# Prompt attention of a hybrid decoder step: mask products in the rounded type, and value products two score blocks behind

## The chip, the cores and the metric

The kernel runs on one core of a Trainium2 chip. The metric is the device time of one execution in microseconds. The kernel before took 2216.69 us (median of three runs, 2213.21 to 2216.88).

## The reference

One decoder layer is computed for a prompt of 1024 tokens and for 8 sequences of 8 new tokens that attend to 8192 cached ones each. The part that the change touches is the causal attention of the prompt, 8 heads with query and key width 96 (64 + 32 rotary) and value width 64, in float32:

```python
s = jnp.einsum('bqhd,bkhd->bhqk', qi, k, preferred_element_type=jnp.float32) * MLA_SCALE
qpos = start + jnp.arange(Q_BLOCK)
s = jnp.where(kpos[None, :] <= qpos[:, None], s, NEG)
pr = jax.nn.softmax(s, axis=-1)
return jnp.einsum('bhqk,bkhd->bqhd', pr.astype(v.dtype), v)
```

Beside it the step has a gated linear attention, a latent attention of the 64 new tokens over the paged cache, an output projection, a gated MLP with a short convolution and a last gated projection.

## The kernel before, in words

**Precision.** A float32 factor is kept as two halves of a rounded 32-bit type that TensorE multiplies in one pass: `split` (L114 to L117) rounds on ScalarE (L115) and subtracts on VectorE or GpSimd (L116). A product is the sum of three (`mm3`, L138 to L141): high by high, low by high, high by low.

**Stages.** Up to about 640 us the prompt's projections and its gated linear attention run; from there to about 1053 us the prompt attention; then the output projection, the MLP and the last projection. Beside all of the first two runs the *cache stream* (`cache_stream`): 64 blocks of 1024 cached tokens, in each of which TensorE transposes the latents (L522, tile `ctp`), multiplies them into keys for 8 heads and the absorbed queries (L139 to L141, tile `ks`: two groups of three products for 128 tokens), ScalarE squares the keys (L560, `csq`) and copies scores (L562, `sn`), VectorE sums (L565), GpSimd scales, and TensorE sums the values (L646, `cpv`).

**What sets the order.** The cache stream and the dense work are Python generators. The dense one yields costs, the main loop draws a cache step each time that its due time is reached (`PACE`), and 95 cache steps are drawn before the dense work ends, in the kernel before and in the changed one. The remaining cache steps are drawn together with the output projection. What is recorded in this way is then ordered on each engine by a scheduler when the program is built; an engine then works through its queue in that order, and the first instruction that waits holds all behind it.

**Prompt attention.** It has 16 units: a head `h` and a half `g` of 512 queries. `prepare` makes a unit's operands: `operands` turns q and k (L1263) for a new head, `shifts` multiplies scores once in the high halves (L1279), adds the mask of the diagonal block as a product of an identity with a mask matrix (L1281) and takes the row maximum on VectorE (L1282), `rows` turns the maxima into an extra row of q (L1292). `values` then goes over blocks `j` of 128 keys, 4 of them for g = 0 and 8 for g = 1: three score products (L1308, L1309, L1312) into the tile `S`, with the mask product (L1311) in the four diagonal blocks, the exponential on ScalarE (L1316, `p`), the rounded half `ph` on VectorE or ScalarE in turn (L1317), the rest `pl` on GpSimd (L1318), and one block later the products with the values into `o`: L1323, L1324 (from `ph`) and L1326 (from `pl`); the first block's `pl` comes last, in L1330. `both` draws the values of one unit and the preparation of the next in turn. The tiles `t`, `S` and `o` of the attention share three PSUM banks (`psD`) with the other dense work.

The mask products go over 16 units x 4 diagonal blocks, twice: 64 in L1281 and 64 in L1311, 128 in all. Their factors are in bfloat16, those of all the products around them are of the rounded type.

Of the kernel before, what the change touches and what calls it, by code (L numbers as in the profile page):

```python
# [8 lines left out]
F32 = mybir.dt.float32  # L9
F32R = mybir.dt.float32r  # L10
BF16 = mybir.dt.bfloat16
I32 = mybir.dt.int32
AF = mybir.ActivationFunctionType
ALU = mybir.AluOpType
# [4 lines left out]
P = 128  # L19
# [16 lines left out]
NEG = -1e30  # L36
# [8 lines left out]
def step_kernel(ctx: ExitStack, tc: tile.TileContext, A):  # L45
    nc = tc.nc
    pe, act, dve, pool, sp = nc.tensor, nc.scalar, nc.vector, nc.gpsimd, nc.sync
# [9 lines left out]
    ident = ctile([P, P], F32, "ident")  # L57
# [131 lines left out]
    def pat(kind):  # L189
        return psD.tile([P, 512], F32, tag="d", name=kind)  # L190
# [1035 lines left out]
    def prompt_attention(ap):  # L1226
# [9 lines left out]
            return ld  # L1236

        ld = {0: load(0)}
        identb = ap.tile([P, P], BF16, name="identb", tag="identb", bufs=1)
        pool.tensor_copy(identb, ident)  # L1240
        masks = []
        for nm, sg in (("maskq", 1), ("maskk", -1)):
            m = ap.tile([P, P], BF16, name=nm, tag=nm, bufs=1)
            pool.memset(m, 0.0)
            pool.affine_select(m, m, pattern=[[-sg, P]], compare_op=ALU.is_ge, fill=NEG, base=0, channel_multiplier=sg)
            masks.append(m)
        maskq, maskk = masks
        qk, vo = [], []
# [20 lines left out]
        def shifts(h, g):  # L1269
            tr = qk[h % 2]  # L1270
            mx = ap.tile([P, 4, 2], F32, tag="amx", name="amx")
            for ii in range(4):
                i = 4 * g + ii
                qs = slice(i * P, (i + 1) * P)
                for j in range(g + 1):
                    kw = (ii + 1) * P if j == g else 512
                    S = pat("t")
                    k0 = j * 512
                    pe.matmul(S[:, 0:kw], tr["qh"][0:96, qs], tr["kh"][0:96, k0:k0 + kw], start=True, stop=j < g)  # L1279
                    if j == g:  # L1280
                        pe.matmul(S[:, kw - P:kw], identb, maskq, start=False, stop=True)  # L1281
                    dve.tensor_reduce(mx[:, ii, j:j + 1], S[:, 0:kw], AX.X, ALU.max, negate=True)  # L1282
                yield 0.06 * (i + 1)
            if g == 1:
                dve.tensor_tensor(mx[:, :, 0], mx[:, :, 0], mx[:, :, 1], ALU.min)
            return mx
# [9 lines left out]
        def values(h, g):  # L1296
            tr = qk[h % 2]
            v = vo[h % 2]
            o = pat("o")
            nj = 4 * g + 4  # L1300
            pls, q = {}, []
            for j in range(nj + 1):
                if j < nj:
                    c0 = max(0, j - 4 * g) * P
                    ks = slice(j * P, (j + 1) * P)
                    qs = slice(g * 512 + c0, g * 512 + 512)
                    S = pat("S")
                    pe.matmul(S[:, c0:], tr["kh"][:, ks], tr["qh"][:, qs], start=True, stop=False)  # L1308
                    pe.matmul(S[:, c0:], tr["kh"][:, ks], tr["ql"][:, qs], start=False, stop=False)  # L1309
                    if j >= 4 * g:  # L1310
                        pe.matmul(S[:, c0:c0 + P], identb, maskk, start=False, stop=False)  # L1311
                    pe.matmul(S[:, c0:], tr["kl"][:, ks], tr["qh"][:, qs], start=False, stop=True)  # L1312
                    p = ap.tile([P, 512], F32, tag="p", name="p", bufs=3)
                    ph = ap.tile([P, 512], F32R, tag="ph", name="ph", bufs=3)
                    pl = ap.tile([P, 512], F32R, tag="pl" if j else "pl0", name="pl", bufs=3 if j else 2)
                    act.activation(p[:, c0:], S[:, c0:], AF.Exp)  # L1316
                    (dve.tensor_copy if j % 2 else act.copy)(ph[:, c0:], p[:, c0:])  # L1317
                    pool.tensor_tensor(pl[:, c0:], p[:, c0:], ph[:, c0:].bitcast(F32), ALU.subtract)  # L1318
                    q.append((j, c0, ph, pl))
                    yield 0.65  # L1320
                if j > 0:
                    jj, c0, ph, pl = q.pop(0)
                    pe.matmul(o[:, c0:], v[:, jj, 0:128], ph[:, c0:], start=jj == 0, stop=False)  # L1323
                    pe.matmul(o[0:64, c0:], v[:, jj, 128:192], ph[:, c0:], start=False, stop=False)  # L1324
                    if jj > 0:
                        pe.matmul(o[:, c0:], v[:, jj, 0:128], pl[:, c0:], start=False, stop=False)  # L1326
                    else:
                        pl0 = pl
                    yield 0.6
            pe.matmul(o, v[:, 0, 0:128], pl0, start=False, stop=True)  # L1330
            r = ap.tile([64, 512], F32, tag="ar", name="ar")
            act.activation(r, o[64:128, :], AF.Ln)
            act.activation(r, r, AF.Exp, scale=-1.0)
            dve.tensor_tensor(r, o[0:64, :], r, ALU.mult)
            sp.dma_start(doT[512 + h * 64:512 + (h + 1) * 64, g * 512:(g + 1) * 512], r)
            yield 0.2
# [926 lines left out]
```

## Time and profile before

| | us |
|---|---|
| runs, median (lowest to highest) | 2216.69 (2213.21 to 2216.88) |
| profiled execution, first to last instruction | 2211.1 |
| TensorE busy in it | 2126.7 (96%) |
| VectorE, ScalarE, GpSimd busy | 1668.4, 1366.7, 1233.9 |
| mask products, first to last | 656.8 to 1047.5 |

The page gives for the profiled execution only its span; the runs' times include what lies before the first and behind the last instruction, so their median lies 5.6 us above the span. A matmul's row in the profile is longer than its share of the engine, since matmuls overlap: what one costs is read from the distance of the starts.

### The profile page before, as it was taken

Reading aid. Unit: us, or ns where it says so; the run is one execution under the profiler, and the core shown is the slowest. Engines: PE = TensorE matmul, PEld = TensorE weight load, DVE = VectorE, ACT = ScalarE, POOL = GpSimd, SP = SyncE. Lnnn points to the kernel's source line nnn. Section 1 sums busy time; section 2 is a strip of 40 time slices with the busy share of each in tenths; the row PEclk is TensorE's granted clock in tenths of the full one; section 3 lists DMA queues with packets and bytes.
Section 4 is the critical chain, followed back from the end, with each engine's and each line's share of the span. In section 5 each row is a group of like instructions: output and inputs, shape, how many; then the busy total and the mean of one; then the engine's idle time right before and its main releaser. Section 6 shows DMA issues by size and latency. Waiting matters only on the chain.

```text
span 2211.1 us, 38379 instructions
## 1 busy us (share of the span) xinstructions
PE 2126.7 (96%) x13460; PEld 1927.2 (87%) x13460; DVE 1668.4 (75%) x2551; ACT 1366.7 (62%) x3724; POOL 1233.9 (56%) x1330
## 2 busy tenths in 40 slices
PE   7999989999999999999999997999999999999999
PEld 6889978878888888887898875999999999888899
DVE  4775667467788888887888788888888886887642
ACT  5676766777778888887777766333333333534631
POOL 5675668576777777778455557756566562011100
PEclk9999999999999999999999998999999999999999
DMA  5343235412342222221522222332232325777321
GB/s 185 106 144 108 78 119 156 141 54 69 105 120 61 63 74 61 61 56 46 171 77 69 74 77 82 101 102 90 92 95 91 101 91 191 240 218 237 101 71 39
DMA packets 204418, 233.07 MB, mean 105 GB/s; under 512 B 42422, under 2 KB 146339, under 8 KB 204227
## 3 DMA queue, kind: packets, MB, share of 16 engines
q1 hardware_dynamic: 188259, 179.49, 26.0%
q0 software_dynamic: 14736, 46.67, 7.4%
q10 hardware_dynamic: 1232, 4.46, 0.5%
q8 instruction: 108, 1.77, 0.3%
q14 instruction: 83, 0.68, 0.1%
HBM read 188.00 MB, written 42.52 MB: 104 GB/s over the span
## 4 chain that ended last, share of the span: by engine, by line
PE 79%; DVE 7%; ACT 5%; DMA 3%; POOL 3%; issue 2%; SPq 0%; DVEq 0%; POOLq 0%; ACTq 0%
PE ps_gu L140 7%; PE ps_gu L141 7%; PE ps_gu L139 7%; PE ks L139 5%; PE ks L141 4%; PE ks L140 4%; PE ps_dn L140 3%; PE ps_dn L141 3%; PE ps_dn L139 3%; PE cpv L646 2%; PE ctp L522 2%; PE ps_lt L278 2%; PE ps_pj L139 2%; DVE css L565 1%; PE ps_pj L140 1%
## 5 line engine op out<-in xcount | busy, mean ns | idle before, releaser
L560 ACT ACTIVATE csq<-ks 128x256 f32<-128x256 f32 x1040 | 392.7, 400 | 91.1 <-PE ks L141 80.2
L565 DVE TENSOR_REDUCE css<-csq 128x16 f32<-128x1024 f32 (+1 forms) x264 | 315.7, 1196 | 61.2 <-ACT csq L560 58.2
L115 ACT CAST wh<-st 128x512 fp32r<-128x512 f32 x176 | 108.4, 619 | 189.0 <-PE ps_gu L140 168.7
L139 PE MATMUL ks<-mv0h,cTh 128*128 128x320 f32 (+1 forms) x520 | 171.0, 331 | 8.8 <-ACT sn L562 4.6
L139 PE MATMUL ks<-mv1h,cTh 128*128 128x320 f32 (+1 forms) x520 | 169.6, 328 | 7.8 <-ACT sn L562 3.5
L605 POOL TENSOR_TENSOR chl<-craw,chl 128x1024 fp32r<-128x1024 f32 x64 | 141.6, 2213 | 55.2 <-ACT chl L603 53.0
L140 PE MATMUL ks<-mv1l,cTh 128*128 128x320 f32 (+1 forms) x520 | 153.1, 296 | 0.0
L140 PE MATMUL ks<-mv0l,cTh 128*128 128x320 f32 (+1 forms) x520 | 152.0, 294 | 0.0
L141 PE MATMUL ks<-mv0h,cTl 128*128 128x320 f32 (+1 forms) x520 | 147.6, 297 | 0.9 <-DVE cTl L116 0.8
L141 PE MATMUL ks<-mv1h,cTl 128*128 128x320 f32 (+1 forms) x520 | 148.0, 298 | 0.1
L116 DVE TENSOR_TENSOR wl<-st,wh 128x512 fp32r<-128x512 f32 x132 | 119.0, 903 | 26.3 <-ACT wh L115 26.3
L631 POOL TENSOR_TENSOR phl<-sn,phl 128x512 fp32r<-128x512 f32 (+1 forms) x64 | 85.5, 1335 | 84.8 <-ACT phl L630 84.3
L116 POOL TENSOR_TENSOR wl<-st,wh 128x512 fp32r<-128x512 f32 x44 | 69.4, 1578 | 102.9 <-ACT wh L115 102.9
L140 PE MATMUL ps_dn<-o 128*128 128x512 f32 x308 | 120.1, 390 | 0.4 <-DVE o L116 0.4
L141 PE MATMUL ps_dn<-o 128*128 128x512 f32 x308 | 120.2, 390 | 0.0
L116 DVE TENSOR_TENSOR cTl<-ctp,cTh 128x512 fp32r<-128x512 f32 (+1 forms) x136 | 90.0, 662 | 37.8 <-ACT cTh L115 36.8
L139 PEld LDWEIGHTS ks<-mv0h,cTh 128*128 128x128 f32 x520 | 97.9, 188 | 23.2 <-ACT sn L562 9.4
L562 ACT COPY sn<-ks 128x64 f32<-128x64 f32 x520 | 116.7, 224 | 0.0
L139 PEld LDWEIGHTS ks<-mv1h,cTh 128*128 128x128 f32 x520 | 99.0, 190 | 20.1 <-ACT sn L562 7.9
L1318 POOL TENSOR_TENSOR pl<-p,ph 128x512 fp32r<-128x512 f32 (+1 forms) x96 | 97.5, 1020 | 30.3 <-DVE ph L1317 21.2
L139 PE MATMUL ps_dn<-o 128*128 128x512 f32 x308 | 112.1, 390 | 0.0
L141 PE MATMUL ps_gu<-xrh,wl 128*128 128x320 f32 x352 | 108.7, 309 | 0.0
(670 smaller groups left out, 7871.4 us busy)
## 6 DMA issues: line engine op xcount, KB each, us to landing
raw<-ds SPq DMA_DIRECT2D x77, 256.0 KB
raw<-ffn_w_down SPq DMA_DIRECT2D x66, 256.0 KB
stage<-w_in SPq DMA_DIRECT2D x48, 256.0 KB
st<-ffn_w_gate SPq DMA_DIRECT2D x44, 256.0 KB
st<-ffn_w_up SPq DMA_DIRECT2D x44, 256.0 KB
wr<-ffn_w_down SPq DMA_DIRECT2D x44, 256.0 KB
ds<-cv SPq DMA_DIRECT2D x21, 512.0 KB
oraw<-doT SPq DMA_DIRECT2D x16, 256.0 KB
```

The costliest lines, as they stand in the source:

```text
L115: cast = act.copy(hi, src)
L116: res = (lo_eng or dve).tensor_tensor(lo, src, hi.bitcast(F32), ALU.subtract)
L139: pe.matmul(ps, ah, bh, start=first, stop=False)
L140: pe.matmul(ps, ah, bl, start=False, stop=False)
L141: return pe.matmul(ps, al, bh, start=False, stop=last)
L278: pe.matmul(ps, x, w, start=first, stop=last)
L560: act.activation(sq[:, f * 256:f * 256 + 256], ks[:, 0:256], AF.Square)
L562: act.copy(o.sn[:, g0 + i, :], ks[:, 256:320])
L565: dve.tensor_reduce(o.ss[:, g0 + i + 1 - n:g0 + i + 1, :].rearrange("p i h -> p (i h)"), sq2[:, :n].rearrange("p i (h n) -> p (i h) n", n= ...
L605: pool.tensor_tensor(ch[:, c0:c1, 128:256], src, ch[:, c0:c1, 0:128].bitcast(F32), ALU.subtract)
L631: pool.tensor_tensor(phl[:, :nt, 64:128], sb, phl[:, :nt, 0:64].bitcast(F32), ALU.subtract)
L1318: pool.tensor_tensor(pl[:, c0:], p[:, c0:], ph[:, c0:].bitcast(F32), ALU.subtract)
```

## The change

The identity and the two mask matrices become tiles of the rounded type (`identr`, `maskq`, `maskk`). Each mask is first made on GpSimd in a float32 tile `mraw`, of which there is one buffer, and then copied. The mask products themselves stay where they stand in the program. In `values` the loop runs one step further, and a block's value products follow two blocks behind its scores; `ph` and `pl` get four buffers instead of three (`p` keeps three).

```diff
-        identb = ap.tile([P, P], BF16, name="identb", tag="identb", bufs=1)
-        pool.tensor_copy(identb, ident)
+        identr = ap.tile([P, P], F32R, name="identr", tag="identr", bufs=1)
+        pool.tensor_copy(identr, ident)
         for nm, sg in (("maskq", 1), ("maskk", -1)):
-            m = ap.tile([P, P], BF16, name=nm, tag=nm, bufs=1)
-            pool.memset(m, 0.0)
-            pool.affine_select(m, m, pattern=[[-sg, P]], compare_op=ALU.is_ge, fill=NEG, base=0, channel_multiplier=sg)
+            raw = ap.tile([P, P], F32, name="mraw", tag="mraw", bufs=1)
+            m = ap.tile([P, P], F32R, name=nm, tag=nm, bufs=1)
+            pool.memset(raw, 0.0)
+            pool.affine_select(raw, raw, pattern=[[-sg, P]], compare_op=ALU.is_ge, fill=NEG, base=0, channel_multiplier=sg)
+            pool.tensor_copy(m, raw)
...
-                        pe.matmul(S[:, kw - P:kw], identb, maskq, start=False, stop=True)
+                        pe.matmul(S[:, kw - P:kw], identr, maskq, start=False, stop=True)
...
-            for j in range(nj + 1):
+            for j in range(nj + 2):
...
-                        pe.matmul(S[:, c0:c0 + P], identb, maskk, start=False, stop=False)
+                        pe.matmul(S[:, c0:c0 + P], identr, maskk, start=False, stop=False)
...
-                    ph = ap.tile([P, 512], F32R, tag="ph", name="ph", bufs=3)
-                    pl = ap.tile([P, 512], F32R, tag="pl" if j else "pl0", name="pl", bufs=3 if j else 2)
+                    ph = ap.tile([P, 512], F32R, tag="ph", name="ph", bufs=4)
+                    pl = ap.tile([P, 512], F32R, tag="pl" if j else "pl0", name="pl", bufs=4 if j else 2)
...
-                if j > 0:
+                if j > 1:
                     jj, c0, ph, pl = q.pop(0)
```

Lines behind L1247 stand two further down in the changed kernel (L1281 becomes L1283).

The scheduler orders the whole stretch from the first mask product to some way into the output projection anew. Three places on TensorE follow; `ks`, `ctp`, `csr`, `cpv`, `mt` and `crp` are tiles of the cache stream, `ps_dn` of the output projection.

The preparation of the last unit, before: its maxima's score products, while the last unit but one multiplies its values.

```order
L1279 MATMUL t<-kh_9446,qh_9444 128x512
L1279 MATMUL t<-kh_9446,qh_9444 128x256
L1281 LDWEIGHTS identb
L1281 MATMUL t<-maskq,identb 128x128
L1323 MATMUL o<-ph,vo_9448 128x512
L1324 MATMUL o<-ph,vo_9448 64x512
L1279 MATMUL t<-kh_9446,qh_9444 128x512
L1323 MATMUL o<-ph,vo_9448 128x384
L1324 MATMUL o<-ph,vo_9448 64x384
L1279 MATMUL t<-kh_9446,qh_9444 128x384
L1281 LDWEIGHTS identb
L1281 MATMUL t<-maskq,identb 128x128
```

The same place in the changed kernel:

```order
L1281 MATMUL t<-kh_9450,qh_9448 128x512
L139 MATMUL ks<-mv1h,cTh 128x320
L140 MATMUL ks<-mv1l,cTh 128x320
L141 MATMUL ks<-mv1h,cTl 128x320
L139 MATMUL ks<-mv1h,cTh 128x256
L140 MATMUL ks<-mv1l,cTh 128x256
L141 MATMUL ks<-mv1h,cTl 128x256
L1281 MATMUL t<-kh_9450,qh_9448 128x256
L1283 MATMUL t<-maskq,identr 128x128
```

Two groups of cache products now stand between two score products that stood side by side. Over the last three units, counted from one L1330 to the next, the program before has 86, 6 and 9 `ks` products, the changed one 72, 69 and 27. Behind the attention's last product and ahead of the first product of the output projection it had 51 `ks` products and now has 90.

The values of the last unit, before:

```order
L1308 MATMUL S<-qh_9444,kh_9446 128x512
L1309 MATMUL S<-ql_9445,kh_9446 128x512
L1312 MATMUL S<-qh_9444,kl_9447 128x512
L1323 MATMUL o<-ph,vo_9448 128x512
L1324 MATMUL o<-ph,vo_9448 64x512
L1326 MATMUL o<-pl,vo_9448 128x512
```

and in the changed kernel:

```order
L1310 MATMUL S<-qh_9448,kh_9450 128x512
L1311 MATMUL S<-ql_9449,kh_9450 128x512
L1313 MATMUL S<-maskk,identr 128x128
L1314 MATMUL S<-qh_9448,kl_9451 128x512
L1328 MATMUL o<-pl,vo_9452 128x512
L1325 MATMUL o<-ph,vo_9452 128x512
L1326 MATMUL o<-ph,vo_9452 64x512
```

Before, a block's `pl` followed its `ph` in one go, behind the next block's scores; now the `pl` product of one block is followed by the `ph` products of the next, and more score products lie ahead of both.

On GpSimd at the start of the attention, the changed kernel has these rows between the first fills and the cache stream's next large subtraction (L605); before, both masks were filled and cut ahead of L592:

```order
L592 TENSOR_TENSOR sn<-sn,cy 128x512
L116 TENSOR_TENSOR vo_9444<-ldv,vo_9444 128x8x64
L1247 CAST maskq<-mraw 128x128
L631 TENSOR_TENSOR phl<-sn,phl 128x9x64
L594 TENSOR_TENSOR sn<-sn,sr 128x512
L1245 MEMSET mraw 128x128
L1246 AFFINE_SELECT mraw<-mraw 128x128
L1247 CAST maskk<-mraw 128x128
```

Each mask now ends in a copy, and the second is made only when the first has left `mraw`.

## The prediction

> **What bounds the kernel now.** I read the page's busy shares and its chain first, then the stages by windows, then the waits and groups of the stage that the change touches.
>
> ```profile
> PE 2126.7 (96%) x13460; PEld 1927.2 (87%) x13460; DVE 1668.4 (75%) x2551; ACT 1366.7 (62%) x3724; POOL 1233.9 (56%) x1330
> PE 79%; DVE 7%; ACT 5%; DMA 3%; POOL 3%; issue 2%; SPq 0%; DVEq 0%; POOLq 0%; ACTq 0%
> ```
>
> TensorE is busy for 96% of the span, and 79% of the chain that ended last is its own. So a change gains what it takes off TensorE's queue or out of its holes. The share is an average; the attention's own stage is read from windows (columns: length, then busy time of PE, PEld, DVE, ACT, POOL with counts, granted clock, DMA share, GB/s).
>
> ```profile
> 656.00:1018.00 362.00, 355.00 (x2455) 311.24 (x2455) 303.66 (x495) 316.66 (x948) 271.96 (x270) 1.00 0.23 65
> 1000.00:1020.00 20.00, 20.00 (x139) 17.27 (x138) 17.86 (x28) 16.96 (x56) 14.71 (x16) 1.00 0.21 61
> 1020.00:1030.00 10.00, 7.59 (x41) 5.94 (x40) 6.57 (x12) 4.51 (x10) 7.81 (x13) 0.85 0.06 14
> 1030.00:1040.00 10.00, 8.78 (x45) 7.04 (x45) 4.57 (x10) 7.15 (x15) 7.63 (x8) 0.84 0.26 66
> 1040.00:1050.00 10.00, 10.00 (x60) 8.12 (x60) 6.01 (x8) 6.78 (x14) 9.38 (x9) 0.97 0.11 29
> 1052.60:1062.20 9.60, 8.14 (x56) 7.25 (x55) 7.48 (x10) 9.40 (x34) 0.78 (x4) 1.00 0.39 116
> ```
>
> Three things stand here. For 362 us the attention and the cache stream fill TensorE (355.0 of 362.0) at full clock. In the 20 us from 1020 on there is a hole: TensorE is busy for 7.59 + 8.78 of 20 us, and the granted clock is 0.85 and 0.84. That is 3.6 us without work, and 15% or so of 16.4 busy us at a lower clock, some 2.5 us: about 6 us in all. And between the attention's end and the first output product (1052.6 to 1062.2) it is ScalarE that is full, 9.40 of 9.60 us, while TensorE is not.
>
> Who made the hole, from the waits of TensorE in 1018 to 1048 (total, times, longest):
>
> ```profile
> PE t L1279 <- DVE amx L1282: 1.6, 2, 0.8
> PE cpv L646 <- POOL phl L631: 0.8, 1, 0.8
> PE S L1309 <- DVE ql L116: 0.8, 1, 0.8
> PE t L1292 <- DVE amx L1285: 0.4, 1, 0.4
> ```
>
> Score products wait for VectorE's maxima, since their PSUM bank must be read first, and nothing else stands between them: the last three units have 86, 6 and 9 `ks` products beside them. The 95 cache steps drawn by then are used up too early.
>
> **The change part by part.** *The mask products.* What one costs in bfloat16, from the order of time; below it what a product of the rounded type of the same width, 128, costs.
>
> ```profile
> 1043.70 0.39 PE L1309 MATMUL S<-ql,kh 97*128 97x512 f32 x1
> 1043.93 0.23 PE L1311 MATMUL S<-maskk,identb 128*128 128x128 bf16 x1
> 1043.97 0.48 PE L1312 MATMUL S<-qh,kl 97*128 97x512 f32 x1
> 1044.29 0.39 PE L1323 MATMUL o<-ph,vo 128*128 128x512 f32 x1
> 1044.52 0.39 PE L1324 MATMUL o<-ph,vo 128*64 128x512 f32 x1
> 1043.47 0.19 PEld L1309 LDWEIGHTS S<-ql,kh 97*128 97x128 f32 x1
> 1043.93 0.10 PEld L1311 LDWEIGHTS <-identb 128*128 128x128 bf16 x1 [0.27 <-issue]
> 1020.03 0.27 PE L1326 MATMUL o<-pl,vo 128*128 128x128 f32 x1
> 1020.14 0.45 PE L1330 MATMUL o<-pl,vo 128*128 128x512 f32 x1
> ```
>
> A product over 512 columns takes 0.23 us of the engine (1043.70 to 1043.93, 1044.29 to 1044.52). From 1043.93 to 1044.29 there are the mask product and L1312's: 0.36 - 0.23 = 0.13 us for the mask. The reason stands in the weight rows: the load of the bfloat16 identity is not issued ahead (idle 0.27, "issue"), it begins when the product before has streamed. The product of the rounded type over 128 columns takes 0.11 us (1020.03 to 1020.14). So 0.02 x 128 = 2.6 us less. Bounds: if the loads of the new identity stood open too, each would be 0.19 long instead of 0.10, 0.09 x 128 = 11.5 us more; if such a product cost only its stream, a quarter of 0.23, 0.06 us, then 0.07 x 128 = 9 us less. I take -2.6, the nearest row: every load of this type around the place runs under the product ahead of it.
>
> Here a rule speaks against the change. The Trainium skill, TensorE: Matmul & The Clock Gate, section "Weight-path perf modes — Fast Weight Load (FWL) and DoubleRow", says that the fast weight load is on for 128 weights of a type other than FP32, about twice as fast as measured there. The two load rows agree with it, 0.10 against 0.19; what it would make of the time is the second rival.
>
> *The masks' making.* On GpSimd, once:
>
> ```profile
> L1240 POOL CAST identb<-ident 128x128 bf16<-128x128 f32 x1 | 0.5, 498 | 0.0
> L1245 POOL TENSOR_SCALAR_AFFINE_SELECT maskq<-maskq 128x128 bf16<-128x128 bf16 x1 | 0.3, 306 | 0.0
> L594 POOL TENSOR_TENSOR sn<-sn,sr 128x512 f32<-128x512 f32 x1 | 1.3, 1281 | 0.0
> ```
>
> Two copies more, 2 x 0.5 = 1.0 us, beside the same fills and cuts, on an engine with 271.96 of 362 us busy. The first mask is ready later, since L592 and a subtraction of the values (about as long as L594, 1.3 us) now stand ahead of its copy; nine to fifteen cache products, each 0.12 to 0.15 us, have been set ahead of L1283 for it. Between 0 and 1.6 us; I take +0.5. The cover is the cache stream's products; without them TensorE would stand for the whole 1.6 us with three banks held.
>
> *Value products a block later.* What they wait for now, over the attention:
>
> ```profile
> L1323 PEld LDWEIGHTS o<-ph,vo 128*128 128x128 f32 x96 | 18.4, 191 | 3.1 <-DVE ph L1317 1.1 <-DVE ar L1334 0.4 <-ACT p L1316 0.4
> L1326 PEld LDWEIGHTS o<-pl,vo 128*128 128x128 f32 x80 | 15.4, 193 | 1.6 <-POOL pl L1318 0.7
> L1318 POOL TENSOR_TENSOR pl<-p,ph 128x512 fp32r<-128x512 f32 x48 | 62.1, 1297 | 12.5 <-ACT ph L1317 6.6 <-DVE ph L1317 5.5
> L1317 ACT CAST ph<-p 128x512 fp32r<-128x512 f32 x32 | 20.2, 632 | 0.2
> L1317 DVE CAST ph<-p 128x512 fp32r<-128x512 f32 x16 | 12.5, 780 | 4.3 <-ACT p L1316 4.2
> L1316 ACT ACTIVATE p<-S 128x512 f32<-128x512 f32 x48 | 29.0, 604 | 8.5 <-PE S L1312 6.4 <-POOL sn L592 0.9 <-POOL pl L1318 0.2
> ```
>
> Exponential, rounding and subtraction of a wide block take 0.60 + 0.63 to 0.78 + 1.30 = 2.5 to 2.7 us one behind the other. Already the cache products hide nearly all of it: the weight loads of the value products stood idle for 3.1 + 1.6 = 4.7 us in 16 units, and 1.1 + 0.4 + 0.7 = 2.2 us of that is put down to `ph`, `p` and `pl`. All of it gone would be 4.7; a loss is possible, since `o` keeps its bank a block longer and leaves two of three for `t` and `S`: a wait of a unit's length of L1279 <- DVE amx (0.8 us) in a few units, +2. I take -1.5.
>
> *What the new order does to the hole.* The last three units get 72, 69 and 27 `ks` products instead of 86, 6 and 9. 69 products at 0.12 to 0.15 us are some 9 us of cover for the unit in which the hole lies. The last unit stays thinly covered. Of the 6 us I take 5 back; bounds 0 and 7.
>
> *Where the cover comes from.* Behind the attention 90 `ks` products instead of 51 now stand ahead of the output projection's first. There nothing but cache work is in the queue, and ScalarE sets the pace:
>
> ```profile
> L560 ACT ACTIVATE csq<-ks 128x256 f32<-128x256 f32 x16 | 6.0, 398 | 0.0
> L562 ACT COPY sn<-ks 128x64 f32<-128x64 f32 x8 | 1.8, 224 | 0.0
> ```
>
> For six `ks` products ScalarE needs 2 x 0.398 + 0.224 = 1.02 us; TensorE needs 3 x 0.12 + 3 x 0.147 = 0.80 (the cadence of 256 and 320 columns by the 0.23 of 512: 0.115 and 0.144). The 39 products more are 6.5 such sets: 6.5 x 0.22 = 1.4 us by these rows alone. ScalarE also has the transposes' casts and the probabilities there, so it may be double; as the row of 1052.6 to 1062.2 shows, TensorE had 8.14 of 9.60 us, a loss of 15%, and a stretch some 10 us longer would lose 1.5 more. The upper bound is that ScalarE falls behind as well for the output weights' casts: 5. I take +2.5.
>
> Sum: -2.6 + 0.5 - 1.5 - 5 + 2.5 = -6.1 us. Against the profiled execution's span of 2211.1 that makes 2205.0. The median of the runs lies 5.6 us above that span, so 2216.7 - 6.1 = 2210.6 is the time to expect.
>
> **The rivals.** *The cover is only moved.* The hole closes, and the whole 5 us come back in the stretch of pure cache work, where ScalarE is full; the deeper values bring nothing, since scheduled order had given them room already. Left is -2.6 + 0.5 = -2.1: 2214.6. For it: ScalarE's 9.40 of 9.60 us, and 4.5 us of the waits in the attention not being of the values. Against it: in the hole ScalarE had 11.7 of 20 us only, so its work is done earlier there than before.
>
> *The identity's load stands open (slower).* It begins in the attention, at each of the 128 mask products, if the order in which PE's sequencer issues them, and not the type, keeps the load from being issued ahead; then -2.6 becomes +11.5 and the sum is 0.5 - 1.5 - 5 + 2.5 + 11.5 = +8.0: 2224.7. Against it: the loads of L1309 and L1312 directly beside it are under other products. For it only the two lengths.
>
> *A new hole.* The whole stretch is ordered anew; one hole like that of 1020 to 1040 in another place costs 6 us and leaves 2216.6, two leave 2222.6. Against it: no unit ahead of the last has fewer than 45 `ks` products beside it, where the hole had 6 and 9.
>
> *More than I count.* Hole, clock and waits of the values go wholly: -2.6 - 4.7 - 7 + 1.4 = -12.9: 2203.8.
>
> **How the numbers follow.** Forecast 0.52, moved cover 0.22, open loads 0.08, a new hole 0.10, more 0.08. What a measurement of this kernel can tell from no change is about 0.2%, 4.4 us: faster means under 2212.3, slower over 2221.1. The forecast's own range, 2206 to 2214, lies by about nine tenths below 2212.3, 0.47, with the 0.08 of the last and a little of the second rival 0.57. Slower: open loads 0.08 and most of the new hole's, 0.15. The rest, 0.28, is no difference. The range goes from 2202 to 2222: it holds the forecast, the moved cover, one new hole, and nearly all of the greater gain; the open loads lie outside.
>
> **What would show it.** The windows from the attention's last 30 us show TensorE at 9.5 of 10 us or more and a clock of 1.00 if the hole is closed. The starts around L1313 tell the mask's price: 0.11 if I am right, 0.20 or more if the load stands open. The window between the last L1332 and the first L1436 shows the moved cover: ScalarE full and TensorE under 85%. The weight loads' idle time at L1325 and L1328 should fall from 4.7 us to about 3. I am wrong if the hole is closed and the time is within 2 us of before, or if L1281 waits for VectorE in other units for more than the 1.6 us here.

## The result, and the profile after

The changed kernel takes 2220.8 us (median of 20 runs, 2216.3 to 2226.7), the kernel before 2216.2 (20 runs on the same chip, 2212.7 to 2222.5): a ratio of 1.0017, 95% interval 1.0011 to 1.0024. It is slower, by some 4 us, where 6 us less were predicted.

The two profiled executions are not medians: the one of before is 3.0 us below its median, the one of after took 2223.9 us, 3.0 above. So their stages differ by 11 us in sum, not by 4.6, and what a stage shows is confirmed below by timed runs. (The page's span lies some 2 us under the time of its own run; the 5.6 that the prediction, and the section on the time before, took for this was mostly the low run.)

Of the page of after: busy time by engine, and the engines' shares of the chain that ended last.

```profile
PE 2128.3 (96%) x13460; PEld 1940.2 (87%) x13460; DVE 1676.5 (75%) x2551; ACT 1364.7 (61%) x3724; POOL 1233.1 (55%) x1332
PE 78%; DVE 9%; ACT 5%; DMA 3%; POOL 2%; issue 2%; SPq 0%; DVEq 0%; POOLq 0%; ACTq 0%
```

These shares tell nothing: 96% before and after. The windows of after do (length, then busy time of PE, PEld, DVE, ACT, POOL with counts, clock, DMA share, GB/s):

```profile
656.00:1018.00 362.00, 351.55 (x2413) 317.83 (x2413) 302.96 (x489) 306.55 (x911) 264.29 (x265) 1.00 0.22 61
1018.00:1037.30 19.30, 19.23 (x127) 17.00 (x126) 14.47 (x21) 16.60 (x48) 17.29 (x18) 1.00 0.14 42
1037.30:1050.00 12.70, 9.08 (x61) 7.57 (x59) 10.76 (x17) 11.74 (x37) 8.00 (x13) 0.99 0.45 143
1050.00:1060.00 10.00, 3.68 (x17) 3.71 (x18) 1.72 (x3) 1.34 (x5) 2.33 (x2) 0.50 1.01 389
1060.00:1070.70 10.70, 8.75 (x60) 7.66 (x60) 9.42 (x15) 8.50 (x30) 7.14 (x9) 1.00 0.96 290
```

The attention's last 19.3 us are full at full clock: the old hole is closed, as predicted. Its last product now comes at 1037.3 instead of 1052.5. Behind it the stretch up to the first output product lasts 33.4 us instead of 9.8, and in the 10 us from 1050 on TensorE has 3.68 us of work at a clock of 0.50. ScalarE, whose pace the prediction took for the limit there, is busy for 11.74 + 1.34 + 8.50 = 21.6 of the 33.4 us: it is not full. The waits of TensorE from 1037 to 1071 name the cause (total, times, longest):

```profile
PE ctp L522 <- DMA craw<-cache_ckv,idx: 8.6, 2, 8.3
PE ks L139 <- ACT sn L562: 2.4, 3, 1.6
PE ks L139 <- ACT csq L560: 0.8, 1, 0.8
```

Its row in TensorE's timeline (start, length, and in brackets the idle time before it and what ended it):

```profile
1056.32 1.09 PE L522 MATMUL ctp<-ident,craw 128*128 128x128 f32 x4 [8.34 <-DMA craw<-cache_ckv,idx]
```

The gather of the next cache block comes late. GpSimd issues it, and SP's loads for the output projection start at the same time (timelines of GpSimd and of SP's queue, same columns):

```profile
1043.54 1.16 POOL L490 CAST qbd1h<-qr 32x64 fp32r<-32x64 f32 x3 [3.16 <-issue]
1044.78 2.33 POOL L491 TENSOR_TENSOR qbd1l<-qr,qbd1h 32x64 fp32r<-32x64 f32 x4
1047.38 0.97 POOL L473 DMA_INDIRECT craw<-cache_ckv,idx  x1 [0.27 <-POOL qbd1l L491]
1045.87 1.07 SPq L1555 DMA_DIRECT2D h<-x_prompt  x2
1047.94 4.26 SPq L1555 DMA_DIRECT2D h<-x_prompt  x6
```

The view of the tile `craw` from 1000 to 1075 has the time from issue to landing:

```profile
DMA to landing us min/median/max: 4.1/4.9/8.8
```

A gather lands 4.9 us after its issue as a rule, this one after 8.8.

**Where TensorE's time went.** For the experiments one measure is used throughout. A product's own share is worked out from rows like those of the prediction: 0.23 us for 512 columns, so 0.45 ns a column, but not under 0.118 us behind a load of 128 weights (0.136 for a bfloat16 mask). What the distances between successive starts are longer than that, shorter ones set off, is *lost*. A lower granted clock counts as lost too. Summed over five stages of each profiled execution, in us:

| kernel | to 800 | 800 to 1018 | 1018 to attention's end | to the first output product | to the first MLP product | sum |
|---|---|---|---|---|---|---|
| before | 10.9 | 10.8 | 9.0 | 2.5 | 44.6 | 77.8 |
| after | 17.9 | 11.2 | 0.5 | 16.5 | 42.8 | 88.9 |

The hole gave back 8.5. The stretch behind the attention took 14.0, and the attention's first third 7.0, of which nothing stood in the prediction. The products' own shares became some 2 us shorter (cheaper masks).

The measure is rough. Taken as a stage's length less its products' shares, an entry comes out up to 3 us lower (to 800 us, before has 9.6 and after 16.4). The clock adds to that. In after the granted clock is 0.50 for 3.4 us from 657.3 on, which is 1.7 of the 7.0 us. The run with pace 1.030 below, in the order of before at that place, has such a dip too (from 657.5), and before has none. Differences of 2 us between two rows therefore say little. The other 5 us fit TensorE's waits by name from 656 to 800: 3.7 us in before, 9.4 in after, of these 6.0 for VectorE.

### The profile page after: what moved, and what is told of

Same layout as the page of the kernel before. It is cut to its first block, busy times and chain, and to the rows that moved or that the text cites. A ratio compares the mean times of both kernels' runs of the same rounds, so it can differ in the third digit from the quotient of the medians.

```text
span 2222.0 us, 38385 instructions
## 1 busy us (share of the span) xinstructions
PE 2128.3 (96%) x13460; PEld 1940.2 (87%) x13460; DVE 1676.5 (75%) x2551; ACT 1364.7 (61%) x3724; POOL 1233.1 (55%) x1332
## 4 chain that ended last, share of the span: by engine, by line
PE 78%; DVE 9%; ACT 5%; DMA 3%; POOL 2%; issue 2%; SPq 0%; DVEq 0%; POOLq 0%; ACTq 0%
PE ps_gu L139 7%; PE ps_gu L141 7%; PE ps_gu L140 7%; PE ks L139 5%; PE ks L141 4%; PE ks L140 4%; PE ps_dn L140 3%; PE ps_dn L141 3%; PE ps_dn L139 3%; PE cpv L646 2%; PE ctp L522 2%; DVE css L565 2%; PE ps_lt L278 2%; PE ps_pj L139 2%; PE ps_pj L140 1%
## 5 line engine op out<-in xcount | busy, mean ns | idle before, releaser
L605 POOL TENSOR_TENSOR chl<-craw,chl 128x1024 fp32r<-128x1024 f32 x64 | 141.3, 2207 | 60.8 <-ACT chl L603 57.1
L631 POOL TENSOR_TENSOR phl<-sn,phl 128x512 fp32r<-128x512 f32 (+1 forms) x64 | 85.2, 1332 | 62.0 <-ACT phl L630 61.5
L592 POOL TENSOR_TENSOR sn<-sn,cy 128x512 f32<-128x512 f32 (+1 forms) x64 | 70.2, 1098 | 72.8 <-DVE cy L590 62.4
```

The source lines that it names most:

```text
L592: pool.tensor_tensor(snv, snv, y[:, :nt].rearrange("p i h -> p (i h)").unsqueeze(2).broadcast_to([P, nt * 8, 8]), ALU.mult)
L605: pool.tensor_tensor(ch[:, c0:c1, 128:256], src, ch[:, c0:c1, 0:128].bitcast(F32), ALU.subtract)
L631: pool.tensor_tensor(phl[:, :nt, 64:128], sb, phl[:, :nt, 0:64].bitcast(F32), ALU.subtract)
```

## The experiments

Each was timed in alternation with the kernel before; ratios are against that, with their 95% intervals.

### One part at a time, order left to the scheduler

Masks alone: the change with the loop and the buffers as before.

```diff
-            for j in range(nj + 2):
+            for j in range(nj + 1):
...
-                if j > 1:
+                if j > 0:
```

> The masks in the rounded type alone, values one block behind as before. Collision theory (the loss sits behind the attention's end, where the residual rows' loads meet a cache gather): the order at that place stays as before (0 and 9 ks products beside the last two units, 51 behind the attention), so only the price of the mask products is left: 128 x 0.02 us, 2213 to 2215, against 2216.2 of before. Rival (the type itself costs: its weight load is twice as long, 0.19 against 0.10 us): slower than before by 3 us or more, 2219 or above.

Measured 2226.7 us, 1.0043 (1.0028 to 1.0058): 10 us slower. Depth alone: masks in bfloat16, loop and buffers as in the change.

> Value products two blocks behind and four buffers alone, masks in bfloat16. Collision theory: the last units get cover (42 and 63 ks products), the attention ends earlier beside the cache stream, 72 ks products stand behind it, and a gather meets the rows' loads there: slower than before by 2 to 8 us, 2218 to 2224, with a wait of ctp for a gather of several us. Rival (the type costs): within 2 us of before, 2214 to 2218.

Measured 2226.0 us, 1.0041 (1.0027 to 1.0055), 9 us slower. The masks alone are where the rival has them, and both lie above what the collision theory gives. Each part alone costs twice what both cost together, so no sum of two prices explains it. Both are ordered anew as a whole, and in both TensorE loses more up to 800 us: 19.5 and 16.6 instead of 10.9.

### The row loads

The changed kernel, and the kernel before, with four of the eight loads of the residual's rows made to wait for the first output units.

```diff
-                    for t in range(NT):
+                    for t in range(4):
...
+                    if g == q == 0:
+                        for t2 in range(4 + t, NT, 4):
+                            row = sp.dma_start(hrows(t2), A["x_prompt"][0, t2 * P:(t2 + 1) * P, :]).ins
+                            tc.add_manual_dep(row, z["chain"].name, ...)   # waits for the unit's last product
```

> The changed kernel, but the residual rows of the second half of the tokens (4 of 8 loads of 512 KB) are loaded one by one behind the first four units of the output projection, each waiting for such a unit's last product, instead of all at once. Order of TensorE up to the first output product is the same. Collision theory: the wait of ctp for its gather (8.3 us in the changed kernel's profile) falls to 4 us or less, and with it the stretch at half clock: 2212 to 2217, 4 to 9 us faster than the changed kernel. Rival (ScalarE's pace over 90 ks products makes the loss there): within 2 us of the changed kernel, 2219 to 2223.

> The kernel before with the same later loads of four residual rows. Collision theory: there no gather is in flight when the rows are loaded, nothing to gain: within 2 us of before, 2214 to 2218. If the rows' loads also hurt before in some other way: 3 us or more faster.

Measured 2240.7 us, 1.0104 (1.0089 to 1.0119), against both theories; and 2216.9, 1.0002 (0.9991 to 1.0013), as expected. In the first the gather's wait is still there (waits of TensorE, 1045 to 1110):

```profile
PE ctp L522 <- DMA craw<-cache_ckv,idx: 8.7, 2, 8.4
```

and with half the row loads the gather still takes 8.9 us to land, with the DMA engines' share at 0.93 to 1.05 from 1055 to 1065. So this run does not test the collision: the four rows and the other loads were enough to fill the DMA engines. Its 20 us come mostly later. Up to the first MLP product TensorE loses some 14 us more than in after, and in SP's queue the late rows wait 16.1 us for the output units, with other loads behind them:

```profile
1091.90 7.90 SPq L1569 DMA_DIRECT2D h<-x_prompt  x3
```

Whether these waits in SP's queue cost the time is not shown: in after SP's queue also has issues that stand for 13.7 and 28.6 us there, and this run's order is a new one too.

### Holding the order

From here on the order is no longer left to chance. The program is recorded twice. The first recording is scheduled freely; in the second, each engine's instructions are tied one behind the other, without a wait, in the order of the first:

```python
for e, seq in follow.items():                # seq: the engine's order in the first recording
    for a, b in zip(seq, seq[1:]):
        tc.add_manual_dep(at[e, b], at[e, a].name, <order only>)
```

**Rounded masks in the order of before**, with the two copies that the change brings (here with two buffers for the float32 tile):

```diff
+    _, order = trace(BF16)              # the kernel before
+    return trace(F32R, follow=order)    # with rounded masks
```

> Masks in the rounded type, value products one block behind, and every engine's instructions held in exactly the order of the kernel before (the two copies that make the masks are the only instructions more). Theory 'the masks are cheaper, and it is the new order that costs': 128 mask products at 0.017 us less (starts 0.118 to 0.120 us apart in the changed kernel, 0.136 in the one before) are 2.2 us, less up to 0.5 for the copies: 2213.5 to 2215. Rival 'the rounded mask itself costs, by what it does to its neighbours', which would also explain the 10 us that the masks alone lost: 2220 or more.

**The mirror**, bfloat16 masks in the order of the changed kernel:

```diff
+    _, order = trace(F32R)              # the changed kernel
+    return trace(BF16, follow=order)    # with bfloat16 masks
```

> The mirror: the changed kernel with every engine's order held, but the masks in bfloat16 again, made without the copies. Theory 'cheaper masks, dearer order': the 2.2 us come back on top of the changed kernel's 2220.8, so 2222 to 2224. Rival 'the rounded mask costs': the time falls below 2219.

Measured 2222.3 us, 1.0029 (1.0016 to 1.0042), and 2223.3 us, 1.0032 (1.0020 to 1.0044). The mirror is as expected. The first is as its rival has it, and its trace says why:

```profile
663.43 0.28 POOL L1249 CAST maskq<-mraw 128x128 fp32r<-128x128 f32 x1
663.77 0.90 PE L1285 MATMUL t<-maskq,identb 128*128 128x128 f32 x3 [4.00 <-POOL maskq L1249]
```

The copies were free to move and came behind three operations of GpSimd (1.07, 1.25 and 1.39 us); the first mask product waited 4.0 us, and the granted clock was 0.50 for 6.8 us from 661.5 on, over 4.6 us of work, so some 2 us more. So it looks to be the making and not the price. The next run tests this without copies: the cut writes the rounded mask itself.

```diff
+            raw = ap.tile([P, P], F32, name="raw" + nm, tag="raw" + nm, bufs=1)
-            pool.memset(m, 0.0)
+            pool.memset(raw, 0.0)
-            pool.affine_select(m, m, ...)
+            pool.affine_select(m, raw, ...)
```

> Every engine held in the order of the kernel before, masks in the rounded type as in the last such run, but the cut writes the rounded mask itself, so that there are no copies: GpSimd has as many instructions as before, and the first mask is ready as early as before. In the run with copies TensorE stood 4.0 us for maskq. Theory 'the price is a gain, the copies were the loss': 128 x 0.017 = 2.2 us less than the kernel before, 2213 to 2215. Rival 'the rounded mask costs by itself': 2217 or more.

Measured 2215.0 us, 0.9996 (0.9987 to 1.0005): 1 us less: no loss as with the copies, and between 2.9 us gained and 1.1 lost. The weight loads of the masks by shape, over the attention, first of before, then of this run (busy, mean ns, idle before them):

```profile
L1311 PEld LDWEIGHTS <-identb 128*128 128x128 bf16 x64 | 6.3, 98 | 7.6 <-issue 6.9
L1281 PEld LDWEIGHTS <-identb 128*128 128x128 bf16 x64 | 6.1, 97 | 6.7 <-issue 4.5
```

```profile
L1313 PEld LDWEIGHTS S<-maskk,identb 128*128 128x128 f32 x64 | 12.2, 191 | 0.7
L1283 PEld LDWEIGHTS t<-maskq,identb 128*128 128x128 f32 x64 | 12.2, 192 | 0.7
```

The load takes twice as long, but is issued ahead and stands under the product before it: 14.3 us of idle loads became 1.4. That refutes the rival of the open load. Whether the bfloat16 load stands open for its type, or for the change of type between neighbours, was not tried. In the trace of after a mask product in a run of 128-column products takes 0.11 to 0.12 us, and the median over the 89 masks that stand between wider products is 0.119, where before has 0.136:

```profile
1031.69 0.28 PE L1311 MATMUL S<-ql,kh 97*128 97x128 f32 x1
1031.81 0.28 PE L1313 MATMUL S<-maskk,identr 128*128 128x128 f32 x1
1031.92 0.28 PE L1314 MATMUL S<-qh,kl 97*128 97x128 f32 x1
```

### One instruction moved

The changed kernel in its own order; only the late gather is moved on GpSimd's queue.

```diff
  DMA krraw<-cache_krope,idx
  DMA craw<-cache_ckv,idx
+ DMA craw<-cache_ckv,idx
  CAST qbd1h<-qr x4
  TENSOR_TENSOR qbd1l<-qr,qbd1h x4
- DMA craw<-cache_ckv,idx
```

> The changed kernel with every engine's order held, but for one instruction: GpSimd issues the last gather of latents ahead of the four casts and four subtractions of qbd1 instead of behind them, so some 3 to 4 us earlier and ahead of the eight row loads. Theory 'the new hole behind the attention is this gather's collision with the row loads': TensorE's wait of 8.3 us at the transposes of ctp falls to under 2 and the time to 2214 to 2216. Rival 'the stretch is bounded by something else (ScalarE's squares, the DMA engines at a share of 1.0), and the wait only moves': 2219 to 2222.

Measured 2217.9 us, 1.0005 (0.9996 to 1.0013), 2.9 us under the changed kernel. Of this run, the gather on GpSimd, and TensorE's waits from 1036.6 to 1064.7:

```profile
1044.24 1.01 POOL L473 DMA_INDIRECT craw<-cache_ckv,idx  x1 [4.86 <-DVE sl L116]
```

```profile
PE ctp L522 <- DMA craw<-cache_ckv,idx: 1.8, 2, 1.5
PE ks L139 <- ACT sn L562: 2.1, 2, 1.6
PE cpv L646 <- POOL phl L631: 1.6, 1, 1.6
```

The gather is issued 3.1 us earlier and lands after 5.1 us at most instead of 8.8, and the wait falls from 8.6 us to 1.8: more than the earlier issue alone would give. So a collision with the loads is shown. By the ratios it is worth 2.7 us, somewhere between 0.3 and 5. But the stretch still loses 11.2 us where that of before loses 2.5 (table below), in several waits on the cache stream's other engines and at a clock of 0.50 for 6.8 us. Half of the expected 6 us came.

### A new order without any of the change

Masks in bfloat16 and values one block behind, as before, but the masks are made through one float32 tile and a copy, as in the change:

```diff
+            raw = ap.tile([P, P], F32, name="mraw", tag="mraw", bufs=1)
             m = ap.tile([P, P], BF16, name=nm, tag=nm, bufs=1)
-            pool.memset(m, 0.0)
-            pool.affine_select(m, m, ...)
+            pool.memset(raw, 0.0)
+            pool.affine_select(raw, raw, ...)
+            pool.tensor_copy(m, raw)
```

> The kernel before, masks still bfloat16 and values one block behind; only the masks are made as in the change, through a float32 tile of one buffer and a copy, with the order left to the scheduler: no product changes its price, and GpSimd has some 1 us more, yet the whole attention is ordered anew (81, 54, 78, 48, 96, 72 ... cache products beside the units instead of 96, 72, 72, 54, 75, 69 ...). Theory 'any new order of this stretch costs, and the order before is a better one than the scheduler gives on average': 2219 to 2227. Rival 'it is the rounded type or the depth of the values': within 2 us of the kernel before, 2214 to 2218.

And the buffers alone:

```diff
-                    ph = ap.tile([P, 512], F32R, tag="ph", name="ph", bufs=3)
-                    pl = ap.tile([P, 512], F32R, tag="pl" if j else "pl0", name="pl", bufs=3 if j else 2)
+                    ph = ap.tile([P, 512], F32R, tag="ph", name="ph", bufs=4)
+                    pl = ap.tile([P, 512], F32R, tag="pl" if j else "pl0", name="pl", bufs=4 if j else 2)
```

> The smallest part of the change alone: four buffers for the halves, bfloat16 masks, values one block behind, order left to the scheduler. No product more or less and the same counts of cache products beside each unit (96, 72, 72, 54 ... 86, 6, 9), but single instructions change places from the attention's start on. Theory 'a new order costs through its small waits even with the same cover': 2218 to 2224. Rival 'only large moves of the cover cost': 2214 to 2218.

Measured 2228.6 us, 1.0055 (1.0042 to 1.0068), and 2223.2 us, 1.0030 (1.0018 to 1.0042): 12 and 6 us slower, with the very same products at the same price. The second has even the same number of cache products beside each unit and behind the attention, and nearly all of its loss lies behind the attention (14.4 us lost instead of 2.5). Two long waits stand there (TensorE, 1050 to 1080):

```profile
PE ctp L522 <- DMA craw<-cache_ckv,idx: 4.6, 1, 4.6
PE ks L139 <- ACT cTh L115: 4.2, 1, 4.2
```

The first is not a collision: this gather lands 4.6 us after its issue, as usual, but it is issued late, behind an operation of VectorE. So these two fresh orders cost by themselves, and more than any part of the change was priced at.

The changed kernel, free order, with the masks cut without copies, as in the run above (0.6 us of GpSimd less):

> The changed kernel, its order left to the scheduler, with the masks cut straight into the rounded type (no copies, no shared float32 tile). The only difference is 0.6 us of GpSimd, yet the attention is ordered anew once more: 49 and 48 cache products beside the last two units in place of 69 and 27, and 39 behind the attention in place of 90. Theory 'what the change costs lies in the order that it happens to get, above all in the bare stretch behind the attention': with half the stretch 2210 to 2216. Rival 'the depth of the values costs by itself (a bank less for the preparation)': 2219 to 2226.

Measured 2219.8 us, 1.0023 (1.0012 to 1.0034): 39 cache products behind the attention instead of 90, and no gain clear of the noise; it is where the rival has it. Its stretch waits for other things (TensorE, 1048 to 1071):

```profile
PE cpv L646 <- POOL phl L631: 4.7, 1, 4.7
PE ks L141 <- DVE cTl L116: 1.5, 1, 1.5
```

### Another pace

The kernel before, with another pace of the cache stream in the attention:

```diff
-PACE = [1.41, 1.088, 1.601, 1.168, 1.142, 0.708, 1.035, 1.027]
+PACE = [1.41, 1.088, 1.601, 1.168, 1.142, 0.708, 1.030, 1.027]
```

> The kernel before, nothing changed but the cache stream's pace in the attention, 1.030 for 1.035: the order is the same up to the last fifth of the attention, and the last two units get 30 and 13 cache products beside them in place of 6 and 9. Theory 'the old hole at 1020 to 1040 is worth 5 us of its own': 2210 to 2213. Rival 'a closed hole only moves the wait behind the attention, as it did in the changed kernel': 2215 to 2218.

The same order, held, with rounded masks cut directly:

> The order of the run with pace 1.030, held on every engine, with rounded masks written by the cut. If the mask's price and the hole add up: 2 us less than that run, 2208 to 2211. If one of the two is not real, within 1 us of the better of them.

Measured 2210.4 us, 0.9976 (0.9965 to 0.9986), and 2211.9 us, 0.9975 (0.9964 to 0.9986). Both are faster than either kernel of the case. The two expected us of the masks do not show, but against each other the two runs are good to some 3 us only. The 5 us are as expected in size, but not where expected. Windows of the run with pace 1.030:

```profile
1020.00:1030.00 10.00, 9.50 (x64) 8.22 (x64) 8.05 (x14) 8.40 (x26) 7.94 (x14) 1.00 0.14 45
1030.00:1040.00 10.00, 7.38 (x50) 6.06 (x49) 8.39 (x17) 6.32 (x17) 9.11 (x13) 0.99 0.22 64
1040.00:1050.00 10.00, 9.67 (x50) 7.91 (x50) 4.58 (x9) 8.13 (x16) 9.16 (x9) 0.84 0.13 33
```

TensorE has 16.9 of the 20 us, against 16.4 before: the hole is hardly smaller. But cache products worth some 7 us, by the shares above, were drawn out of the output projection into the attention, and in the projection the loss fell by 6.4 (44.6 to 38.2); why, was not followed up. The time of a hole is not what filling it brings; that depends also on the place that the filling is taken from.

### Depth alone

In the held order of before, on TensorE only, each block's value products are moved behind the scores of the block after the next (masks in bfloat16, three buffers):

```diff
  S(j+1) products
- o(j) products
  S(j+2) products
+ o(j) products
```

> Value products two blocks behind, alone, in the order of the kernel before: on TensorE each block's value products are moved behind the scores of the block after the next (a unit's first ones also behind the preparation's tiles that are recorded ahead of them), and nothing else on any engine moves; masks in bfloat16, three buffers. Theory 'depth neither gains nor costs, the free order does': 2214 to 2218, within 2 us of the kernel before. Rival 'depth costs by itself, a bank less for the preparation, and this is the 7 us of the attention's first third': 2219 to 2225. The forecast's own step, 1.5 us gained, would be 2213 to 2215.

And both parts of the change in the order of pace 1.030:

> Both parts of the change, rounded masks and values two blocks behind, laid into the order of the run with pace 1.030 (2210.4), in which the old hole is filled and the stretch behind the attention stays short; three buffers, masks written by the cut. Theory 'the change itself is nearly free of charge, and its loss is the order that it got': 2208 to 2213. Rival 'depth costs': 2215 to 2222.

Measured 2220.7 us, 1.0015 (1.0006 to 1.0025), and 2215.6 us, 0.9992 (0.9984 to 1.0001). Both are where the rivals have them. Depth costs 3.3 us (1.3 to 5.5) in the one order, and 1.7 parts in a thousand, 3.8 us (0.7 to 6.9), against the run with the same masks in the other. Of the waits of the weight loads, 656 to 1018, first of before, then with depth alone:

```profile
PEld ks L139 <- ACT sn L562: 3.3, 9, 0.7
PEld S L1308 <- DVE amx L1282: 1.9, 3, 0.8
PEld S L1308 <- ACT p L1316: 1.2, 3, 0.5
PEld ks L139 <- ACT cTh L115: 1.2, 2, 0.8
PEld o L1323 <- DVE ph L1317: 0.8, 2, 0.6
PEld ks L141 <- DVE cTl L116: 0.8, 2, 0.5
PEld o L1326 <- POOL pl L1318: 0.7, 1, 0.7
```

```profile
PEld ks L139 <- ACT sn L562: 3.7, 8, 0.7
PEld ks L139 <- ACT cTh L115: 3.4, 4, 1.4
PEld S L1310 <- DVE amx L1284: 3.3, 4, 1.4
PEld ks L141 <- DVE cTl L116: 3.0, 6, 0.7
PEld ks L139 <- ACT csq L560: 1.8, 3, 0.9
PEld o L1327 <- DVE ph L1319: 0.4, 1, 0.4
```

The value products' waits do go, from 2.7 us (the two `o` rows and three more of 0.4) to 0.4. But what stood behind them moves ahead, and that is for the most part the cache stream's products, whose operands come no earlier. Their waits grow: counted in each run from the attention's start, so that a wait of 1.4 us that lies ahead of 656 in before is in, from 6.9 to 11.9 us. The waits of `S` for VectorE's maxima grow by 1.4. In the order of pace 1.030 it is the same: the value products' waits go from 2.4 to 0.4, the cache products' from 6.7 to 12.1. No wait of ScalarE, VectorE or GpSimd for a buffer of the halves is seen, so the three buffers do not seem to be what costs.

All lost times, in the stages of the first table:

| kernel | to 800 | 800 to 1018 | to attention's end | to output | to MLP | sum | ratio |
|---|---|---|---|---|---|---|---|
| before | 10.9 | 10.8 | 9.0 | 2.5 | 44.6 | 77.8 | 1 |
| after | 17.9 | 11.2 | 0.5 | 16.5 | 42.8 | 88.9 | 1.0017 |
| after, gather first | 18.1 | 11.8 | 0.2 | 11.2 | 43.1 | 84.4 | 1.0005 |
| masks alone, free | 19.5 | 14.5 | 10.5 | 2.7 | 46.4 | 93.6 | 1.0043 |
| depth alone, free | 16.6 | 15.9 | 0.5 | 10.5 | 44.1 | 87.6 | 1.0041 |
| masks' making alone, free | 19.3 | 15.1 | 10.0 | 2.5 | 47.0 | 93.9 | 1.0055 |
| buffers alone, free | 13.5 | 10.8 | 10.7 | 14.4 | 41.6 | 91.0 | 1.0030 |
| depth, old order | 12.9 | 15.8 | 8.0 | 2.5 | 45.8 | 85.0 | 1.0015 |
| pace 1.030 | 12.1 | 10.7 | 7.0 | 4.8 | 38.2 | 72.8 | 0.9976 |

Up to 800 us most of the orders that are new from the attention's start lose 16.6 to 19.5 us, also with neither depth nor rounded masks in them. Those that keep the old order there lose 10.9 to 13.2, apart from the run with the late copies. A new order need not lose there: with the buffers alone it is 13.5, and the free order with directly cut masks, which has depth too, loses 2 us more than before. Depth laid into the old order adds 2.0, and 1.7 of that is a dip of the clock to 0.50 at 660.9 that before lacks. The changed order held, with the gather moved, loses 18.1 again. So as far as these runs tell, the 7.0 us that after loses there come with its order and hardly with depth.

Depth's cost in the held orders lies from 800 to 1018: 5.0 us (15.8 against 10.8), and 4.7 in the order of pace 1.030. In the changed kernel's own order that stage loses no more than before, 11.2. So what depth costs there is open: a price found in one order need not hold in another.

## Why the prediction was wrong, step by step

- **Mask products, -2.6 us.** The price was right: 0.119 instead of 0.136, 2.2 us for 128. As time the held orders show 1.2 us (2.9 gained to 1.1 lost) in the old order, about 0 in that of pace 1.030 and 3.3 (0.3 to 6.3) in that of the change, by the mirror: too rough to tell 2.2 from 0, and good enough to refute the rival of the open load.
- **The masks' making, +0.5, bounds 0 to 1.6.** In after no wait for a mask is seen; where the copy stood behind one operation more (L631) it was 4.0 us. The bound holds in the order that it was read from only; it took the cover of one order for a property of the change.
- **Value products later, -1.5, bounds -4.7 to +2.** Wrong in sign in two held orders: +3.3 and +3.8. There the value products' waits went as the step says, but the stall went for the most part to the cache products; the wait for the maxima, in which the step sought it, grew by 1.4 us only. In after itself not even the waits went: where the prediction has the idle time before the value products' loads fall from 4.7 us to about 3, the weight loads by shape, 656 to 1037, show 8.0.

```profile
L1325 PEld LDWEIGHTS o<-ph,vo 128*128 128x128 f32 x96 | 18.1, 189 | 6.3 <-DVE ql L116 2.0 <-DVE ph L1319 1.2 <-DVE amx L1284 0.6
L1328 PEld LDWEIGHTS o<-pl,vo 128*128 128x128 f32 x79 | 14.9, 189 | 1.7 <-POOL pl L1320 1.1
```

- **The hole, -5.** It closed, and TensorE lost 8.5 us less there.
- **Cover moved behind the attention, +2.5, upper bound 5.** This is the step that failed by most: 14.0 in the profile. It went by ScalarE's pace alone, and ScalarE was busy for 21.6 of the stretch's 33.4 us. 5.3 of the 14.0 (2.7 in the timed runs, by the ratios) is the gather's collision with the loads; what is left shows as waits for `sn`, `csq` and `phl` and as work at half the clock. The likely reason, argued and not tested, is that pure cache work behind the attention has no other work to cover its own latencies; and it coincides with the loads of the next stage.
- **A new hole.** It had 0.10, with the argument that no unit is thinly covered; the sum has nothing for it. It is the case that came, in many small waits (7.0 us in the first third, 1.7 of them the clock's) and the one large one behind the attention. Fresh orders without any of the change's products cost 6 and 12 us. With the buffers alone every unit has as many cache products beside it as before, and the loss came all the same: such a count says nothing on whether a product's operand is there.

The time lies just inside the stated range, but that is luck and not the sum's doing: single steps were off by up to 12 us, and in part they made up for each other. Of the moved cover's reasons, the 4.5 us of waits in the attention that are not the values' are in no view; from 656 to 1018 TensorE's waits for other things come to 5.3.

Not settled is how the 4.6 us divide. The gather is worth 2.7, the cheaper masks take off some 2, the closed hole takes off up to 8.5, depth adds between nothing and 3.3, and the fresh order and the rest of the stretch make up the difference. They do not come apart, since a free order changes with every part. All six free orders that are new from the attention's start, the run with late rows aside, are slower than before, by 4 to 12 us, so the order of before is better than what the scheduler gives as a rule. That the loss lies in the order is shown for the edits that change no product; for the change itself it is argued from these.

## What to carry to other kernels

Where a scheduler orders the program, an edit of a microsecond reorders the instructions of some 400 us, and the edit is then compared in two orders, not in two forms: hold the order while judging the edit, and time some neutral edits to learn what a fresh order costs. Moving a waiting product back removes the wait only if the work that moves up in its place has its operands by then. Cover that is moved to the border of two stages can meet the next stage's loads.

## What the runs showed of the hardware

How long VectorE's rounding of a block takes depends on GpSimd. In after the 16 casts of `ph` over 512 columns on VectorE take 0.41 to 0.43 us in the eight cases where no sum or difference of GpSimd is under way, and 0.60 to 2.73 in the eight where one is. The longest, at the place of the longest wait of a value product in the first third:

```profile
739.63 2.73 DVE L1319 CAST ph<-p 128x512 fp32r<-128x512 f32 x1
739.86 2.20 POOL L605 TENSOR_TENSOR chl<-craw,chl 128x1024 fp32r<-128x1024 f32 x1
742.27 0.68 DVE L116 TENSOR_TENSOR ql<-t,qh 96x512 fp32r<-96x512 f32 x1
743.01 0.50 PE L1325 MATMUL o<-ph,vo 128*128 128x512 f32 x1 [1.80 <-DVE ql L116]
```

The cast ends 0.3 us behind GpSimd's subtraction, and `ql` and the value product wait behind it. The Trainium skill, SBUF — State Buffer, section "Who interferes with whom", says that VectorE in its two-port modes and GpSimd share a pair of ports and that the later of the two is blocked until the other has finished. The sixteen casts agree, though in this row the cast's record begins 0.23 us ahead of the subtraction's, and which came first at the ports the trace doesn't tell. An overlap alone does not lengthen the cast: in the free order with directly cut masks two such casts of 0.40 and 0.41 us, at 786.43 and 933.33, lie wholly inside a subtraction of GpSimd that ends 1.16 us behind them. It is a way in which the same instructions in another order take another time; that it makes the first third's loss was not tested.

Also not expected: a gather from GpSimd's queue took 8.8 instead of 4.9 us from issue to landing with the DMA engines' share at 1.01, and TensorE's granted clock was 0.50 over the 10 us of that wait. In all seventeen traces the granted clock is either 1.00 or 0.50, and the stretches at 0.50 last 3.4, 6.8, 10.2, 13.7 or 17.1 us, apart from the one that the end of a trace cuts off.
